# Up projection of a ConvFFN: another order of products, operands, evictions and norm at its border

## The chip, the cores and the metric

The kernel runs on 1 core of one Trainium2 chip. The metric is the device time of one execution in microseconds (us). TensorE (PE, with its weight loads, PEld) multiplies, VectorE (DVE), ScalarE (ACT) and GpSimd (POOL) work elementwise, SyncE (SP) issues most loads. Each engine works through its own queue in order, and semaphores tie the queues together.

## The reference

One layer of a streaming encoder: two kinds of linear attention, an output projection with a residual, a norm, and a gated ConvFFN. The border that this document is on lies between the output projection and the ConvFFN. In 1024 frames of a prompt and 64 of a running stream (T2 = 1088 columns) this is computed there:

```python
x = x + g1 * jnp.einsum('bte,ed->btd', mix, w_out)
h2 = _rmsnorm(x, g_norm_ffn) * (1.0 + sc2) + sh2
a, up = jnp.split(jnp.einsum('btd,df->btf', h2, w_ffn_in), 2, axis=-1)
buf = jnp.concatenate([conv0.astype(a.dtype), a], axis=1)
conv = conv_b + conv_w[0] * buf[:, 0:T]
...
y = jax.nn.silu(conv) * up
x = x + g2 * jnp.einsum('btf,fd->btd', y, w_ffn_out)
```

D_MODEL is 1024, D_FF 2816. All is float32; the kernel gets the precision from matmuls of float32r in three parts (high times high, high times low, low times high), so each operand is cut: ScalarE casts the high half, VectorE subtracts it from the source for the low half (`cut`).

## The kernel before

**Output projection.** The columns are worked off in three chunks (c = 0, 1, 2) of 384, 384 and 320. Chunk by chunk, eight tiles of 128 rows are projected; the result with its residual lies in `hf[0..7]`, eight tiles of 128 x 1088 (in the profile `ab` for 0 to 2, `hf` for 3 to 5, `cv` for 6 and 7). POOL stores each part in DRAM, and the squares are summed in `sqs`.

**Norm.** `norm2` sums the squares over the partitions by a matmul with ones, takes the root on VectorE (`rsqrt`), spreads it over the partitions by three matmuls with the identity, and then scales each tile (VectorE, from PSUM) and adds a bias (ScalarE). It is a generator: for chunks 0 and 1 it runs in steps between the projection's tiles, whenever the program calls `flow.tick()` and a step's delay is over. The chunk that ends last, 2, is normed by explicit calls behind the projection; its columns 256 to 320 have another scale, so each tile takes two instructions on each engine.

**Up projection.** It is a product of blocks with seven products for eight. `hf` is cut in blocks by half of the rows and half of the columns: h11 and h12 are the first and second 544 columns of tiles 0 to 3, h21 and h22 those of 4 to 7. The operands `X[p]` are, in the order of the sums that they need: X1 = h11 and X2 = h21, cut in the norm of chunks 0 and 1; X3 = h22, without a sum; X5 = h12 - h11 (sum 1, in place of h11); X6 = h22 - that (sum 2, in place of h22); X7 = h22 - h12 (sum 3, in place of h12; it must read h22 ahead of sum 2); X4 = (sum 2) - h21 by sum 4, in place of h21. The column at which chunk 1 ends falls into the second half, so sums 1 and 3 have a part of 224 columns that is there after chunk 1 and one of 320 (`edge` to HT) that waits for chunk 2. The 5632 output rows are done in 22 groups q of 2 x 128, the two being of one half each. A product (q, p) is 24 matmuls of 272 columns: four k tiles, three parts, two column halves. Its accumulator is a pair of PSUM banks, `dA` for products 1 and 2, `dX` for the others and for the norm of chunk 2; there are two pairs of each. Products 1 and 2, 6 and 7, 5 and 3 share one accumulator each, and what stands in between is evicted by `evict_in`.

**Weights.** `raw_load` fetches 128 columns of `w_ffn_in` at a time on SP's queue into three buffers; `need_in` forms the weight sums on VectorE and `prep_in` the cut operand of a product, into six slots (`hi` and `lo` by name in turn, whichever half is in them). `prep_to(n)` does that for the first n entries of `steps`.

**Order.** The first entries of `steps` are worked off by a straight list of calls behind the projection, the rest by a loop: prepare weights ahead, `product`, `evict_in`, then parts of the convolution and gate (`run_aux`) within a budget of 2.9 per step. The tiles `ab0` have two buffers; the first one is used for the vectors of the convolution (`ct`, transposed on TensorE in `turn_vectors`), the second and third as the two outputs of q = 0, so that the third takes the first one's place. Each output tile gets two zero columns by POOL when product 1 is evicted.

Of the kernel before, what the change touches and what calls it, by code (L numbers as in the profile page):

```python
# [19 lines left out]
P = 128  # L20
# [173 lines left out]
def stream_step_kernel(  # L194
# [1211 lines left out]
    def sub(out, a, b):  # L1406
        V.tensor_tensor(out=out, in0=a, in1=b, op=ALU.subtract)
# [12 lines left out]
    def parts(c):  # L1420
        return ((0, WID[c], 0),) if c < 2 else ((0, 256, 0), (256, 320, 1))
# [17 lines left out]
    def operand(p, half_k, half_t, pool, a=0, b=HT):  # L1439
        if p not in X:  # L1440
            X[p] = pool.tile([P, 2, 4, HT], F32R, name=f"X{p}", bufs=1)
        t = X[p]
        for i in range(4):
            src = hf[4 * half_k + i][:, half_t * HT + a:half_t * HT + b]
            cut(t[:, 0, i, a:b], t[:, 1, i, a:b], src)
            yield 0.8

    def sums_b(which, a, b, eng=None):

        for i in range(4):  # L1450
            h11, h12 = hf[i][:, a:b], hf[i][:, HT + a:HT + b]
            h21, h22 = hf[4 + i][:, a:b], hf[4 + i][:, HT + a:HT + b]
            if which == 1:
                (eng or V).tensor_tensor(out=h11, in0=h12, in1=h11, op=ALU.subtract)
            elif which == 3:
                sub(h12, h22, h12)
            elif which == 2:
                sub(h22, h22, h11)
            else:
                sub(h21, h22, h21)  # L1460

    def norm2(c, sqs):
# [6 lines left out]
        rstd = rsqrt(vv, 3, "n")  # L1469
        yield 2.5  # L1470
        for j in range(3):
            mm(pn[:, 1, j * P:(j + 1) * P], rstd[:, j:j + 1].broadcast_to([P, P]), ident, True,
               True)
        for k in range(KD):
            for a, b, j in parts(c):
                o = hf[k][:, c * CW + a:c * CW + b]
                V.scalar_tensor_tensor(out=o, in0=o, scalar=A2[:, k, j:j + 1], in1=pn[:, 1, a:b],
                                       op0=ALU.mult, op1=ALU.mult)
                S.activation(out=o, in_=o, func=AF.Identity, bias=B2[:, k, j:j + 1])
            if c < 2:  # L1480
                yield 1.0
            elif k == 3:
                sums_b(1, 2 * CW - HT, HT, G)
        if c < 2:
            yield from operand(1, 0, 0, xap, CW * c, (CW, HT)[c])
            yield from operand(2, 1, 0, xap, CW * c, (CW, HT)[c])
# [84 lines left out]
    for c in range(NC3):  # L1573
# [4 lines left out]
        for n, m in enumerate(M_ORDER[c]):  # L1578
# [112 lines left out]
    def y_sums(q):  # L1691

        i = q // 2
        u0, u1 = abt[q, 0], abt[q, 1]
        b11, b12 = (cvt[i, 0][:, h * 512:h * 512 + 512] for h in range(2))
        b21, b22 = (cvt[i, 1][:, h * 512:h * 512 + 512] for h in range(2))

        def one():
            while small_lo:
# [6 lines left out]
        def two():  # L1706
            sub(u0[:, 512:1024], b22, u0[:, 0:512])
            nc.gpsimd.dma_start(out=d_y[i][:, 4:6], in_=u0[:, 0:1024]
                                .rearrange("p (n t) -> p n t", n=2))
            sub(u1[:, 0:512], u0[:, 512:1024], b21)  # L1710
            nc.gpsimd.dma_start(out=d_y[i][:, 2:4], in_=cvt[i, 1][:, 0:1024]
                                .rearrange("p (n t) -> p n t", n=2))
            nc.gpsimd.dma_start(out=d_y[i][:, 6], in_=u1[:, 0:512])
        aux.extend([("D", one, 1.4), ("D", two, 1.4)])

    def run_aux(budget):
        while aux:
# [22 lines left out]
    def evict_in(q, p):  # L1740
# [103 lines left out]
    prep_to(11)
# [512 lines left out]
```

## Time and profile before

| | us |
|---|---|
| median of 3 runs (1491.54 to 1493.49) | 1491.79 |
| profiled execution, its own time | 1496.77 |
| its span | 1495.0 |
| TensorE busy in the span | 1372.2 (92%) |
| VectorE | 1070.9 (72%) |
| ScalarE | 625.8 (42%) |
| GpSimd | 307.2 (21%) |

All times in the text count from the span's start. The profile tells for each instruction its engine, start and duration, and, where an engine stood idle ahead of it, how long and which engine's work ended that. In names such as `X<-ab,X` the tile written stands ahead of those read. Line 91 is the helper that records every elementwise instruction, line 234 the matmul, line 239 the transpose. PEclk is the share of TensorE's 2.4 GHz that was granted: 1.00 is full clock, 0.50 is 1.2 GHz.

### The profile page before, as it was taken

How to read it: one execution, taken by the hardware profiler on the slowest of the kernel's cores; microseconds unless marked ns; L12 is line 12 of the kernel's file. 1: busy time of each engine (PE TensorE's matmuls, PEld its weight loads, DVE VectorE, ACT ScalarE, POOL GpSimd, SP SyncE). 2: the span in 40 equal slices, each digit the busy share in tenths (PEclk: the TensorE clock that was granted, in tenths of full speed). 3: DMA queues.
4: the chain of work that ended last, by engine and by line, in shares of the span. 5: the costliest groups of instructions: out<-in, count | busy, mean ns of one | idle time of the engine just before them, and what ended most of it. 6: DMA issues, size and time to landing. Idle time of an engine off the chain costs nothing.

```text
span 1495.0 us, 23802 instructions
## 1 busy us (share of the span) xinstructions
PE 1372.2 (92%) x9082; PEld 1277.3 (85%) x9082; DVE 1070.9 (72%) x1992; ACT 625.8 (42%) x1277; POOL 307.2 (21%) x412
## 2 busy tenths in 40 slices
PE   5999888989999998799779999999999999899996
PEld 3788777879988988798769999999999997788875
DVE  6637878967886788646697777777777765568775
ACT  5735434432333223435464444444434444334343
POOL 3335423415242323411110000000000011110010
PEclk9999999999999999899889999999999999999998
DMA  8420102123222222444302422333233338565522
GB/s 255 155 76 4 55 15 75 45 84 100 83 79 86 76 75 62 118 149 139 104 15 72 140 60 76 107 106 98 95 99 106 106 100 289 185 195 184 173 81 113
DMA packets 157977, 158.27 MB, mean 106 GB/s; under 512 B 9738, under 2 KB 128616, under 8 KB 157864
## 3 DMA queue, kind: packets, MB, share of 16 engines
q1 hardware_dynamic: 147303, 120.58, 26.1%
q0 software_dynamic: 10560, 36.18, 7.1%
q8 instruction: 71, 1.16, 0.3%
q14 instruction: 43, 0.34, 0.1%
HBM read 126.80 MB, written 29.93 MB: 105 GB/s over the span
## 4 chain that ended last, share of the span: by engine, by line
PE 56%; DVE 22%; issue 8%; ACT 6%; DMA 2%; POOL 1%; DVEq 0%; ACTq 0%; POOLq 0%
PE dX L234 23%; PE mm L234 10%; PE dA L234 8%; PE mn L234 5%; PE al L234 3%; PE o L234 2%; DVE lo L91 2%; DVE qbd L91 2%; DMA rb<-d_y 2%; DVE acc L91 2%; DVE att L91 1%; ACT hi L91 1%; DVE X L91 1%; PE sc L234 1%; DVE ab L91 1%
## 5 line engine op out<-in xcount | busy, mean ns | idle before, releaser
L234 PE MATMUL dX<-X,lo 128*128 128x272 f32 x1344 | 182.0, 292 | 5.5 <-DVE ab L91 3.4
L234 PEld LDWEIGHTS dX<-X,lo 128*128 128x128 f32 x1344 | 175.6, 191 | 6.6 <-ACT cv L91 3.0
L234 PE MATMUL dX<-X,hi 128*128 128x272 f32 x1296 | 174.8, 291 | 5.0 <-DVE ab L91 2.8
L234 PEld LDWEIGHTS dX<-X,hi 128*128 128x128 f32 x1296 | 168.7, 191 | 5.8 <-issue 2.9
L234 PE MATMUL mm<-act_hi,hi 128*128 128x384 f32 (+1 forms) x480 | 170.8, 356 | 0.3 <-DVE mix L91 0.2
L234 PE MATMUL mm<-act_lo,hi 128*128 128x384 f32 (+1 forms) x480 | 158.9, 331 | 0.1
L234 PE MATMUL mm<-act_hi,lo 128*128 128x384 f32 (+1 forms) x480 | 158.5, 330 | 0.0
L91 ACT CAST hi<-raw 128x512 fp32r<-128x512 f32 (+1 forms) x116 | 91.1, 787 | 78.9 <-DVE raw L91 66.7
L234 PE MATMUL al<-ba,hi 128*128 128x512 f32 x396 | 102.1, 401 | 4.8 <-DVE x L91 4.8
L234 PE MATMUL mn<-lo,hi 128*128 128x512 f32 x396 | 94.6, 395 | 2.7 <-ACT lo L91 2.1
L234 PEld LDWEIGHTS mm<-act_hi,hi 128*128 128x128 f32 x480 | 92.1, 192 | 1.9 <-DVE mix L91 0.5
L234 PEld LDWEIGHTS mm<-act_lo,hi 128*128 128x128 f32 x480 | 91.9, 191 | 0.7 <-POOL act_lo L91 0.3
L234 PEld LDWEIGHTS mm<-act_hi,lo 128*128 128x128 f32 x480 | 91.4, 190 | 0.0
L234 PEld LDWEIGHTS mn<-lo,hi 128*128 128x128 f32 x396 | 74.7, 190 | 19.4 <-ACT lo L91 2.6
L91 DVE SCALAR_TENSOR_TENSOR cv<-ab,cw,cv 128x1088 f32<-128x1088 f32 x44 | 59.3, 1347 | 44.3 <-ACT cv L91 44.3
L234 PEld LDWEIGHTS al<-ba,hi 128*128 128x128 f32 x396 | 72.3, 191 | 20.0 <-DVE x L91 5.9
L234 PE MATMUL mm<-hi,act_hi 128*128 128x256 f32 x288 | 88.3, 307 | 0.3 <-ACT hi L91 0.2
L234 PE MATMUL mm<-lo,act_hi 128*128 128x256 f32 x288 | 82.7, 287 | 3.0 <-DVE lo L91 3.0
L234 PE MATMUL mm<-hi,act_lo 128*128 128x256 f32 x288 | 82.1, 285 | 0.0
L91 POOL TENSOR_TENSOR acc<-acc,prod 128x512 f32<-128x512 f32 x42 | 64.8, 1544 | 81.6 <-ACT prod L91 80.8
L234 PE MATMUL dA<-X,hi 128*128 128x272 f32 x552 | 74.3, 291 | 0.0
L234 PEld LDWEIGHTS dA<-X,hi 128*128 128x128 f32 x552 | 71.8, 191 | 0.0
(352 smaller groups left out, 3091.7 us busy)
## 6 DMA issues: line engine op xcount, KB each, us to landing
raw<-in_w_ffn_in_dram SPq DMA_DIRECT2D x44, 512.0 KB
raw<-in_w_ada_dram SPq DMA_DIRECT2D x32, 512.0 KB
raw<-in_w_in_dram SPq DMA_DIRECT2D x28, 512.0 KB
rw<-in_w_ffn_out_dram SPq DMA_DIRECT2D x51, 256.0 KB
d_y<-cv POOLq DMA_DIRECT2D x22, 512.0 KB, 4.8
rb<-d_y POOLq DMA_DIRECT2D x44, 256.0 KB, 3.8
raw<-in_w_out_dram SPq DMA_DIRECT2D x18, 512.0 KB
wa<-in_w_ada_dram SPq DMA_DIRECT2D x16, 512.0 KB
```

What stands on the lines that cost most here:

```text
L91: return call(*args, **kw)
L234: T.matmul(out, lhsT, rhs, start=start, stop=stop, skip_group_check=more)
```

## The change

The straight list between the projection and the loop is written in another order, and the pieces that it calls are smaller:

- `norm2` falls into `norm_root`, `norm_spread` and `norm_tile`; chunk 2's norm no longer runs as a generator between halves of products.
- `sums_b`, which did four tiles at once, becomes `sum_b` for one tile. `strip(p, i)` makes one tile of an operand: its sum for p = 6 or 4, and its cut.
- The first eight products are (0,1), (1,1), (0,2), (0,3), (0,5), (0,6), (0,7), (0,4) instead of (0,1), (0,2), (1,1), (0,5), (0,3), and the rest. Product (0,3) gets an accumulator of its own, "E", and the eviction of (0,5) adds it.
- The columns `edge` to HT of sum 1 move from POOL to VectorE, those of sum 3 from VectorE to POOL. The parts after chunk 1 are done tile by tile.
- The vectors of the convolution are transposed behind (0,5) instead of in the middle of the first three products.
- Evictions stand ahead of the weights of later products; before the loop weights are made for one product beyond, not three; (0,4) is multiplied in the list, not in the loop; the loop makes two weights at most per step, and in the first sixteen steps one tap of the convolution (cost 1.3 in its budget) is always let through.
- Chunk 0's and 1's norm waits 0.8 instead of 1.0 between tiles, and 0.7 instead of 0.8 between cuts. `y_sums` looks up its tiles when it runs.

```diff
+    def sum_b(which, i, a, b, eng=None):
+        h11, h12 = hf[i][:, a:b], hf[i][:, HT + a:HT + b]
+        h21, h22 = hf[4 + i][:, a:b], hf[4 + i][:, HT + a:HT + b]
+        o, x, y = {1: (h11, h12, h11), 3: (h12, h22, h12), 2: (h22, h22, h11),
+                   4: (h21, h22, h21)}[which]
+        (eng or V).tensor_tensor(out=o, in0=x, in1=y, op=ALU.subtract)
...
+    FIRST = [(0, 1), (1, 1), (0, 2), (0, 3), (0, 5), (0, 6), (0, 7), (0, 4)]
...
+        grp = GROUP[p] if (q, p) != (0, 3) else "E"
+        first = p in (1, 6, 5, 4) or grp == "E"
...
+            if q == 0:
+                V.tensor_tensor(out=view(dst(q, 0, 1)), in0=o, in1=view(dst(q, 0, 1)), op=ALU.add)
...
-    product(0, 1, 0, 2)
-    next(gen)
-    product(0, 1, 2, 4)
-    turn_vectors()
-    evict_in(0, 1)
-    prep_to(6)
-    product(0, 2, 0, 2)
-    all_of(gen)
-    product(0, 2, 2, 4)
-    product(1, 1)
-    all_of(operand(5, 0, 0, xbp))
-    product(0, 5)
-    all_of(operand(3, 1, 1, xbp))
-    evict_in(0, 5)
-    product(0, 3)
-    sums_b(3, edge, HT)
-    sums_b(2, 0, HT)
...
+    def strip(p, i):
+        if p not in X:
+            X[p] = xbp.tile([P, 2, 4, HT], F32R, name=f"X{p}", bufs=1)
+        if p == 6:
+            sum_b(2, i, 0, HT)
+        elif p == 4:
+            sum_b(4, i, 0, HT)
+        half_k, half_t = {5: (0, 0), 3: (1, 1), 6: (1, 1), 7: (0, 1), 4: (1, 0)}[p]
+        cut(X[p][:, 0, i], X[p][:, 1, i], hf[4 * half_k + i][:, half_t * HT:half_t * HT + HT])
...
+    product(0, 1)
+    pn, rstd = norm_root(2, sqs)
+    evict_in(0, 1)
+    need_in(0, 2)
+    product(1, 1)
+    norm_spread(pn, rstd)
+    for i in range(4):
+        norm_tile(2, 4 + i, pn)
+        strip(3, i)
+    product(0, 2)
+    prep_to(4)
+    product(0, 3)
+    for i in range(4):
+        norm_tile(2, i, pn)
+        sum_b(1, i, edge, HT)
+        strip(5, i)
+        sum_b(3, i, edge, HT, G)
+        if i == 0:
+            prep_to(5)
+    evict_in(0, 3)
+    product(0, 5)
     turn_vectors()
...
+    for i in range(4):
+        strip(6, i)
+        if i == 0:
+            prep_to(6)
     evict_in(0, 5)
...
+    product(0, 4)
...
+    prep_to(9)
+    evict_in(0, 4)
...
+    now[0] = len(FIRST) - 1
+    run_aux(1.4)
...
-        cost = prep_to(s + 1 + LA)
+        cost = prep_to(min(n_prep[0] + 2, s + 1 + LA))
...
-        run_aux(2.9 - cost)
+        run_aux(max(2.9 - cost, 1.4 if s < 2 * len(FIRST) else 0.0))
```

In the built order of instructions, TensorE's queue between the projection's last tile and the third product (`ident,ab` is the transpose of the convolution's vectors, `ident,nr` the spread of the norm):

```order
 L239 MATMUL dX<-ident,xr 128x128 x3
-L234 MATMUL dA<-X_7020,hi 128x272 x12
+L234 MATMUL dA<-X_7005,hi 128x272 x24
 L234 MATMUL dX<-ones,sqs 128x1 x3
-L234 MATMUL dA<-X_7020,hi 128x272 x12
-L239 MATMUL dX<-ident,ab_7491 128x88
-L239 MATMUL dX<-ident,ab_7491 128x44
-L234 MATMUL dA<-X_7068,lo 128x272 x12
+L234 MATMUL dA<-X_7005,lo 128x272 x24
 L234 MATMUL dX<-ident,nr 128x128 x3
-L234 MATMUL dA<-X_7068,lo 128x272 x12
```

Whole products stand now on either side of the norm's two matmuls, and the transposes of the vectors are gone from this place.

VectorE's queue where X5 is made, before (the norm of tile 7 of `hf`, the last one, in its two parts, and then X5):

```order
L91 SCALAR_TENSOR_TENSOR cv_6497<-cv_6497,A2_127,dX_7653 128x256 [waits DMASW7_49]
L91 SCALAR_TENSOR_TENSOR cv_6497<-cv_6497,A2_127,dX_7653 128x64
L91 TENSOR_TENSOR X5_7796<-ab_6490,X5_7796 128x544 [waits DMAHW5_49,DMAHW4_49,DMAHW6_49,DMAHW3_49,Activation_49]
L91 TENSOR_TENSOR X5_7796<-ab_6491,X5_7796 128x544 [waits Activation_49]
L91 TENSOR_TENSOR X5_7796<-ab_6492,X5_7796 128x544 [waits Activation_49]
L91 TENSOR_TENSOR X5_7796<-hf_6493,X5_7796 128x544 [waits Activation_49]
```

and after (`hi_7806<-ws` is a low half of the weights):

```order
L91 SCALAR_TENSOR_TENSOR ab_6490<-ab_6490,A2_127,dX_7659 128x256 [waits DMASW2_49]
L91 SCALAR_TENSOR_TENSOR ab_6490<-ab_6490,A2_127,dX_7659 128x64
L91 TENSOR_TENSOR ab_6490<-ab_6490 128x320 [waits Activation_49]
L91 TENSOR_TENSOR X5_7802<-ab_6490,X5_7802 128x544 [waits Activation_49]
L91 TENSOR_TENSOR hi_7806<-ws_7589,hi_7806 128x512 [waits Activation_49]
L91 SCALAR_TENSOR_TENSOR ab_6491<-ab_6491,A2_127,dX_7659 128x256 [waits DMASW1_49]
L91 SCALAR_TENSOR_TENSOR ab_6491<-ab_6491,A2_127,dX_7659 128x64
L91 TENSOR_TENSOR ab_6491<-ab_6491 128x320 [waits Activation_49]
L91 TENSOR_TENSOR X5_7802<-ab_6491,X5_7802 128x544 [waits Activation_49]
```

A tile's scaling, sum and low half follow each other now, and the next tile's scaling stands behind them.

POOL's queue at the same place, after (`ab0_7686` is the second output tile of q = 0; before, the four sums were `ab<-ab` and `hf<-hf`, sum 1):

```order
L91 MEMSET ab0_7684 128x2 [waits Pool_49]
L91 MEMSET ab0_7686 128x2 [waits DMAHW3_49,DMAHW4_49,DMAHW2_49,PE_49]
L91 TENSOR_TENSOR ab_6490<-hf_6494,ab_6490 128x320 [waits DMASW2_49,DVE_49]
L91 TENSOR_TENSOR ab_6491<-hf_6495,ab_6491 128x320 [waits DMASW1_49,DVE_49]
L91 TENSOR_TENSOR ab_6492<-cv_6496,ab_6492 128x320 [waits DMASW0_49,DVE_49]
L91 TENSOR_TENSOR hf_6493<-cv_6497,hf_6493 128x320 [waits DMASW3_49,DVE_49]
```

The sums in this place are now those of sum 3; the fill ahead of them waits for TensorE, that is for the transposes.

## Rows read from the trace of the kernel before

**Rows 1.** Busy us (instructions) of PE, PEld, DVE, ACT, POOL; PEclk, DMA, GB/s

```profile
730.00:745.00 15.00, 9.13 (x42) 8.48 (x41) 9.04 (x28) 4.17 (x10) 1.29 (x4) 0.60 0.09 29
...
760.00:775.00 15.00, 11.80 (x71) 11.40 (x70) 14.93 (x25) 8.54 (x16) 1.22 (x2) 0.77 0.13 36
...
790.00:805.00 15.00, 15.00 (x122) 15.00 (x121) 9.87 (x15) 6.88 (x12) 0.10 (x1) 1.00 0.01 1
```

**Rows 2.** TensorE in order of time: start, us, instruction, count, idle before, releaser

```profile
729.08 1.75 PE L234 MATMUL dA<-X,hi 128*128 128x272 f32 x12
735.77 1.44 PE L234 MATMUL dX<-ones,sqs 128*128 128x1 f32 x6 [4.94 <-DVE sqs L91]
...
739.93 0.61 PE L239 MATMUL dX<-ident,ab 88*128 88x88 f32 x2
...
744.37 0.84 PE L234 MATMUL dX<-ident,nr 128*128 128x128 f32 x3
...
747.61 3.16 PE L234 MATMUL dA<-X,hi 128*128 128x272 f32 x24
...
767.98 5.78 PE L234 MATMUL dX<-X,hi 128*128 128x272 f32 x24 [2.75 <-DVE ab L91]
...
778.43 3.52 PE L234 MATMUL dX<-X,hi 128*128 128x272 f32 x24 [1.50 <-ACT hi L91]
784.74 4.56 PE L234 MATMUL dX<-X,lo 128*128 128x272 f32 x24 [2.79 <-DVE ab L91]
...
798.17 3.17 PE L234 MATMUL dX<-X,lo 128*128 128x272 f32 x24
801.19 3.16 PE L234 MATMUL dA<-X,hi 128*128 128x272 f32 x24
```

**Rows 3.** VectorE in order of time: root of chunk 2 and first scalings

```profile
737.24 0.16 DVE L91 TENSOR_SCALAR vv<-dX 128x3 f32<-128x3 f32 x1 [0.20 <-PE dX L234]
...
739.41 0.16 DVE L91 SCALAR_TENSOR_TENSOR nr<-na,nr 128x3 f32<-128x3 f32 x1
...
745.89 1.84 DVE L91 SCALAR_TENSOR_TENSOR ab<-ab,A,dX 128x256 f32<-128x256 f32 x6 [2.62 <-PE dX L234]
```

**Rows 4.** ScalarE in order of time: the first three tiles' biases

```profile
746.40 2.03 ACT L91 ACTIVATE ab<-ab,B 128x256 f32<-128x256 f32 x6 [3.94 <-DVE ab L91]
```

**Rows 5.** VectorE, 715 to 800, by shape: count, busy us, mean ns, idle before

```profile
L91 DVE TENSOR_TENSOR X<-ab,X 128x544 fp32r<-128x544 f32 x6 | 4.0, 716 | 1.6 <-ACT X L91 1.6
...
L91 DVE TENSOR_TENSOR raw<-raw 128x512 f32<-128x512 f32 x5 | 3.4, 689 | 0.1
...
L91 DVE SCALAR_TENSOR_TENSOR ab<-ab,A,dX 128x256 f32<-128x256 f32 x3 | 1.4, 478 | 2.6 <-PE dX L234 2.6
...
L91 DVE TENSOR_TENSOR ab<-hf,ab 128x320 f32<-128x320 f32 x2 | 0.9, 480 | 0.0
```

**Rows 6.** ScalarE, 715 to 800, by shape, as rows 5

```profile
L91 ACT CAST X<-ab 128x544 fp32r<-128x544 f32 x6 | 3.5, 643 | 0.0
...
L91 ACT ACTIVATE ab<-ab,B 128x256 f32<-128x256 f32 x3 | 1.5, 500 | 3.9 <-DVE ab L91 3.9
...
L91 ACT ACTIVATE ab<-ab,B 128x64 f32<-128x64 f32 x3 | 1.0, 334 | 0.0
```

**Rows 7.** POOL in order of time: second fill and the four sums

```profile
740.61 0.10 POOL L91 MEMSET ab<- 128x2 f32 x1 [4.77 <-PE dX L239]
747.24 2.55 POOL L91 TENSOR_TENSOR ab<-ab 128x320 f32<-128x320 f32 x3 [6.53 <-ACT ab L91]
749.75 0.89 POOL L91 TENSOR_TENSOR hf<-hf 128x320 f32<-128x320 f32 x1
```

**Rows 8.** VectorE in order of time, 601 to 617: alone, then beside POOL's subtractions

```profile
601.48 0.56 DVE L91 TENSOR_TENSOR mix<-mix,gate 128x384 f32<-128x384 f32 x1 [0.96 <-ACT gate L91]
602.30 4.91 DVE L91 TENSOR_TENSOR act_lo<-mix,act_hi 128x384 fp32r<-128x384 f32 x4 [0.26 <-ACT act_hi L91]
```

More of the change, by code (lines that the diff above doesn't have):

```diff
@@ L1445, in operand, with norm_root @@
             cut(t[:, 0, i, a:b], t[:, 1, i, a:b], src)
[L1446 to L1462, printed above, removed]
+            yield 0.7
+    def sum_b(which, i, a, b, eng=None):
[4 more added lines that the diff above has]
+        (eng or V).tensor_tensor(out=o, in0=x, in1=y, op=ALU.subtract)
+    def norm_root(c, sqs):
         pn = pair("dA") if c < 2 else pair("dX")
@@ L1468, in norm2, with norm_spread @@
                         op1=ALU.add)
-        rstd = rsqrt(vv, 3, "n")
-        yield 2.5
+        return pn, rsqrt(vv, 3, "n")
+    def norm_spread(pn, rstd):
         for j in range(3):
@@ L1473, in norm2, with norm_tile @@
                True)
-        for k in range(KD):
[L1475 to L1486, printed above, removed]
+    def norm_tile(c, k, pn):
+        for a, b, j in parts(c):
+            o = hf[k][:, c * CW + a:c * CW + b]
+            V.scalar_tensor_tensor(out=o, in0=o, scalar=A2[:, k, j:j + 1], in1=pn[:, 1, a:b],
+                                   op0=ALU.mult, op1=ALU.mult)
+            S.activation(out=o, in_=o, func=AF.Identity, bias=B2[:, k, j:j + 1])
+    def norm2(c, sqs):
+        pn, rstd = norm_root(c, sqs)
+        yield 2.5
+        norm_spread(pn, rstd)
+        for k in range(KD):
+            norm_tile(c, k, pn)
+            yield 0.8
+        yield from operand(1, 0, 0, xap, CW * c, (CW, HT)[c])
+        yield from operand(2, 1, 0, xap, CW * c, (CW, HT)[c])
         if c == 1:
-            sums_b(1, 0, 2 * CW - HT)
-            yield 1.0
-            sums_b(3, 0, 2 * CW - HT)
+            for i in range(4):
+                sum_b(1, i, 0, 2 * CW - HT)
+                sum_b(3, i, 0, 2 * CW - HT)
+                yield 0.6
     ORD_IN = (1, 6, 5, 2, 7, 3, 4)
-    steps = [(0, 1), (0, 2), (1, 1), (0, 5), (0, 3), (0, 6), (0, 7), (0, 4)]
+    FIRST = [(0, 1), (1, 1), (0, 2), (0, 3), (0, 5), (0, 6), (0, 7), (0, 4)]
+    steps = list(FIRST)
     steps += [(1, p) for p in ORD_IN[1:]]
@@ L1617, in stream_step_kernel @@
                                   .rearrange("j (f p) -> (j f) p", p=P))
-            if c == 2 and n == 5:
+            if c == 2 and n == 6:
                 prep_to(2)
-                need_in(0, 3)
-            if c == 2 and n == 6:
-                prep_to(4)
+                need_in(0, 1)
         if c < 2:
@@ L1694, in y_sums, with blocks @@
         u0, u1 = abt[q, 0], abt[q, 1]
-        b11, b12 = (cvt[i, 0][:, h * 512:h * 512 + 512] for h in range(2))
-        b21, b22 = (cvt[i, 1][:, h * 512:h * 512 + 512] for h in range(2))
+        def blocks():
+            return [cvt[i, n][:, h * 512:h * 512 + 512] for n in range(2) for h in range(2)]
         def one():
+            b11, b12, _, b22 = blocks()
             while small_lo:
@@ L1706, in two @@
         def two():
+            _, _, b21, b22 = blocks()
             sub(u0[:, 512:1024], b22, u0[:, 0:512])
@@ L1725, in run_aux @@
                 last_d[0] = now[0]
+    GROUP = {1: "A", 2: "A", 6: "B", 7: "B", 5: "C", 3: "C", 4: "D"}
     def product(q, p, k0=0, k1=4):
-        grp = {1: "A", 2: "A", 6: "B", 7: "B", 5: "C", 3: "C", 4: "D"}[p]
-        first = p in (1, 6, 5, 4)
+        grp = GROUP[p] if (q, p) != (0, 3) else "E"
+        first = p in (1, 6, 5, 4) or grp == "E"
         if first and k0 == 0:
@@ L1747, in evict_in @@
         have.add(p)
-        o = held[q, {1: "A", 2: "A", 6: "B", 7: "B", 5: "C", 3: "C", 4: "D"}[p]][:, :, 0:HQ]
+        o = held[q, GROUP[p] if (q, p) != (0, 3) else "E"][:, :, 0:HQ]
         cost = 0.75
@@ L1811, in stream_step_kernel @@
     edge = 2 * CW - HT
-    gen = norm2(2, sqs)
-    need_in(0, 2)
-    need_in(0, 4)
-    product(0, 1, 0, 2)
-    next(gen)
-    product(0, 1, 2, 4)
-    turn_vectors()
-    evict_in(0, 1)
-    prep_to(6)
-    product(0, 2, 0, 2)
-    all_of(gen)
-    product(0, 2, 2, 4)
-    product(1, 1)
-    all_of(operand(5, 0, 0, xbp))
-    product(0, 5)
-    all_of(operand(3, 1, 1, xbp))
-    evict_in(0, 5)
-    product(0, 3)
-    sums_b(3, edge, HT)
-    sums_b(2, 0, HT)
-    all_of(operand(6, 1, 1, xbp))
-    evict_in(0, 3)
-    prep_to(7)
+    def strip(p, i):
[7 more added lines that the diff above has]
+        cut(X[p][:, 0, i], X[p][:, 1, i], hf[4 * half_k + i][:, half_t * HT:half_t * HT + HT])
+    prep_to(3)
+    product(0, 1)
+    pn, rstd = norm_root(2, sqs)
+    evict_in(0, 1)
+    need_in(0, 2)
+    product(1, 1)
+    norm_spread(pn, rstd)
+    for i in range(4):
[13 more added lines that the diff above has]
+    product(0, 5)
+    turn_vectors()
+    for i in range(4):
+        strip(6, i)
+        if i == 0:
+            prep_to(6)
+    evict_in(0, 5)
     product(0, 6)
-    all_of(operand(7, 0, 1, xbp))
+    for i in range(4):
+        strip(7, i)
+        if i == 0:
+            prep_to(7)
     evict_in(0, 6)
-    prep_to(8)
     product(0, 7)
-    sums_b(4, 0, HT)
-    all_of(operand(4, 1, 0, xbp))
+    for i in range(4):
+        strip(4, i)
+        if i == 0:
+            prep_to(8)
+    product(0, 4)
     sp = [spp.tile([P, 8, P], F32R, tag="sp", name="sp", bufs=3) for _ in range(3)]
     evict_in(0, 7)
-    prep_to(11)
+    prep_to(9)
+    evict_in(0, 4)
     def spart(f):
```

2 lines of the change are left out of this document (1 added, 1 removed).

## Prediction

> **What bounds the kernel now.** I read the busy shares by stretch first [rows 1]: from 790 us on TensorE is busy all the time at full clock, so whatever the border before it takes is added to the end one for one. In 730 to 745 us TensorE is busy 9.13 of 15 us at a granted 0.60, in 760 to 775 us 11.80 at 0.77, while VectorE is busy 14.93 of 15. The border is therefore VectorE's. Then the matmuls in order of time [rows 2]: product (0,1) begins at 729.08, (1,6), the first of the loop, at 778.43, and (2,1), the first of the third group, at 801.19, behind which products follow each other every 3.02 us. Of these 72.1 us TensorE needs 14 times 3.02, 42.3 us. A wait is dear twice: behind 2.75 us of waiting the 24 matmuls of one product took 5.78 us (the 1.2 GHz level), against 3.16 at 2.4 GHz. The change touches only this stretch; I put it on the same clock, from 729.08 on, and ask when (1,6) and (2,1) begin.
>
> **The start of the norm: earlier by 8.6 us.** Before, the root of chunk 2 begins at 737.24 [rows 3], as its matmul with the ones waited 4.94 us for VectorE, which was making half sums and weights; its spread over the partitions stands behind a half of product (0,2) and comes at 744.37 [rows 2], and the first normed tile at 745.89 [rows 3]. After, the half sums stand some places earlier, in gaps in which VectorE waits for the projection. (0,1) runs 729.08 to 732.4, the ones take 0.7 at full clock (half of their 1.44) to 733.2, and the root takes the 2.35 us of before [rows 3], to 735.6, behind (1,1), which needs no wait and ends at 736.3. With the spread (0.9) the first tile starts at 737.3. TensorE has (0,1), (1,1) and (0,2) done at 740.4, where before it ended the third at 750.8 (747.61 and 3.16).
>
> **The strips: what replaces it.** This is the term that decides. Before, all eight tiles go through VectorE, and ScalarE follows one tile behind: six instructions, three tiles, take 1.84 us [rows 3] and the biases 2.03 [rows 4], so that a tile costs some 0.6 and nobody waits. After, VectorE's queue holds, strip for strip, scaling, (sum,) cut, and each waits for ScalarE's bias or cast of the same strip; both engines work in the order of their queues, so the next strip's scaling can't pass. A strip costs its whole chain, not the larger engine's part. With 0.03 to a hand-over (0.478 [rows 5] from 745.89 ends at 746.37; the bias starts at 746.40 [rows 4]):
> X3: scaling 0.48 (its second part runs beside the first bias), two biases 0.74 (0.50 and 0.33 with the overlap), cast 0.64, low half 0.64 (0.716 less the 0.08 that the next overlaps), hand-overs 0.1 [rows 5, 6]: 2.6, four 10.4, to 747.7.
> Weights of (0,3): difference 0.69, cast 0.62 (by the 0.643 of 544 columns), low half 0.69 [rows 5, 6]: 2.0, to 749.7.
> X5: the same and the sum of 320 columns, 0.48 [rows 5], that now stands on VectorE: 3.1, four 12.4, and the weights' low half 0.6, to 762.7.
> (0,5) does not start with its first strip: its accumulator is the norm's, which the last scaling reads until 760.4. TensorE has stood by then, and I charge it the 5.78 us of the half clock [rows 2]; with the transposes of the vectors (0.6) it ends at 766.8.
> POOL: the fill of the second output tile waits, before as after, for those transposes, since that tile takes their buffer; before, nothing was queued behind it but sums that came 6.53 us later [rows 7]. After, the four sums for X7 stand behind it in POOL's queue, and VectorE's sums for X6 wait for them, as they overwrite what POOL reads. First sum 0.1 and 0.9 later, 767.8: VectorE has idled 5.1 us.
> X6: sum 0.72, cast 0.64, low half 0.64, hand-overs: 2.07, four 8.3, weights 0.6. Beside it run POOL's other three sums. When both engines subtracted at once, four of VectorE's took 4.91 us against 0.56 for one of that width alone [rows 8]; so I add 1.0 (0, if they fit into its waits, to 2.6, three sums of 0.87). To 777.7.
> X7 has no sum, so ScalarE runs ahead: one eviction 0.64, four low halves 2.55, weights 0.6; the eviction of (0,6), two instructions, 1.4. To 782.9.
> X4: like X6, 8.3 and 0.6, to 791.8; eviction of (0,7) 1.4; three sums of weights 2.0; cast and hand-overs 0.65. (1,6) starts at 795.8 against 778.43: **17.4 us later**.
> From below it is 12.3: (0,5) at full clock gives back 2.7, strips without any hand-over 48 times 0.03, POOL's sums the 1.0. From above 22.4: hand-overs of 0.1 add 48 times 0.07, POOL's sums another 1.6.
>
> **The first steps of the loop.** From (1,6) to (2,1) six products took 22.8 us before, 4.6 more than 6 times 3.02: there the weights were late too (2.79 us of waiting ahead of 784.74, then 4.56 us for a product [rows 2]). After, weights are made two to a step, not up to five ahead, and each step must take a tap. From (1,6)'s weights to the eviction that frees the accumulator of (1,4), VectorE has four taps of 1088 columns (1.3 each, twice 0.64), twelve weight instructions (some 0.62), four evictions (0.64) and the seven small ones (1.1): 16.2 us, and waits about 5 for casts and for the convolution's parts on ScalarE: 21.4, against the 19.7 that (1,4) lay behind (1,6). With the half clock for (1,4), 1.4 as at 784.74, that is 3.1 more. Bounds: minus 4.6 (no wait is left) and plus 5.
>
> Moved, and at no cost: the loads of the third and later weights are issued where their buffer comes free and have more time than before, as all is later; chunk 1's shorter pauses fill VectorE's gaps ahead of 729 us, in which TensorE was at the projection's pace (if that cover failed, each 0.1 would be paid once for each tile).
>
> **Sum.** Plus 17.4 plus 3.1: 20.5 us. The profiled execution took 1496.77 (span 1495.0); with it 1517.3. The median of the three is 1491.79, 5.0 below the profiled one; on it the forecast is **1512.3 us**. The parts' own ends are plus 7.7 (12.3 less 4.6) and plus 27.4.
>
> A rule that speaks against my reading: VectorE's four subtractions in 4.91 us [rows 8] beside POOL's. The Trainium skill, "SBUF — State Buffer", section "SBUF: two separate sides", says that a VectorE instruction with two SBUF inputs and a GpSimd one exclude each other for a whole instruction; this trace agrees with it (1.23 us for each instead of 0.56), and by it the term for X6 would be 2.6 rather than 1.0 and the sum 22.1.
>
> **Rivals.** *The strips give work earlier (faster than before).* If the two engines overlapped across strips, a strip would cost VectorE's own part: 1.3 for X3, 1.8 for X5, 1.3 for X6 and X4. X5 would end near 752.8, (0,5) run at full clock, and by the other terms of above (1,6) start at 777.6, 0.8 us sooner; with the loop's 4.6 gone it is 1491.8 less 5.4, **1486**. The place is VectorE's queue between two strips; the sixteen strips of X3, X5, X6 and X4 cost 39.4 us by my count, 2.5 each, and with full clock and no wait in the loop (together 10.4 off 20.5) it turns where their mean falls below 1.8. For it: the norm does come 8.6 us sooner. Against it: the built order, in which each strip's cut is ahead of the next strip's scaling, and VectorE's 14.93 of 15 us [rows 1]. The Trainium skill, "Perfetto Trace Analysis", section "Optimizing Scalar/DVE Operations", says that where these engines are not saturated but cause bubbles elsewhere, breaking up instructions may complete work sooner; that is this rival, and in 760 to 775 us its condition isn't met. 5%.
> *Nothing to be seen (within 0.2%).* X3's and X5's strips overlap (10.4 less), which keeps the full clock for (0,5) (2.7) and leaves no wait in the loop (7.7), and X6's and X4's don't: 20.5 less 20.8, **1491.5**. For and against it stands the same as for the first. 3%.
> *Slower, but half.* Full clock for (0,5) (2.7), and no wait in the loop (3.1 and 4.6), since two weights a step suffice: plus 10.1, **1502**. For it: the wait of 2.79 at 784.74 was of evictions that now come ahead of weights. 12%.
> *Slower by more than 26*, where hand-overs, port and loop all stand at their upper ends: plus 27.4, **1519**. 4%.
>
> **How the numbers follow.** The forecast, slower by 14 to 26, has 76%. A measurement here can tell about 0.2%, 3 us. Faster by more 5%, within it 3%, slower by more 92%. From 1503 to 1518 the range leaves out the faster and the equal case, the lower half of the half case and the last: about 2 in 10.
>
> **What would show it.** In the changed kernel's trace the first normed tile stands near 737 us and the third product's end near 740; then TensorE waits some 9 us for X3. The low halves of X3 follow each other every 2.6 us and those of X5 every 3.1, each behind a wait for ScalarE. POOL's second fill stands behind the transposes, and VectorE waits about 5 us for POOL. (1,6) starts near 796, (2,1) near 822. I am wrong if X3's low halves come every 1.3 us, if (0,5) starts ahead of 757, or if (2,1) starts ahead of 811.

## Result and profile after

| | before | after |
|---|---|---|
| median of 4 runs, us | 1491.66 | 1512.55 (1511.68 to 1513.55) |
| profiled execution, us | 1496.77 | 1511.68 |
| its span, us | 1495.0 | 1509.9 |
| VectorE, ScalarE, GpSimd busy, us | 1070.9, 625.8, 307.2 | 1076.2, 627.1, 307.2 |
| (0,1)'s start to (2,1)'s start, us | 72.1 | 92.8 |

The changed kernel is slower: 1.0136 of the time before, 95% interval 1.0120 to 1.0152, 20.9 us by the medians (of before one more run is in it than ahead of the prediction); in a later group of runs 1.0134 (1.0110 to 1.0158). The spans differ by only 14.9 us. What lies outside of the border explains this: in the profiled execution of before, (0,1) began 2.8 us later (729.08 [rows 2] against 726.29), and the part behind (2,1) took 3.0 us longer (1495.0 less 801.19 against 1509.9 less 819.11). The 2.8 us are not the change's: 2.6 of them are there at the projection's first transposes already, which began at 619.01 and 616.40, and from these to (0,1) the two kernels take 110.1 and 109.9 us. So the border by itself, 20.7 us, is what the medians show, and below every kernel is read by that stretch, from (0,1)'s start to (2,1)'s. To set a time of after beside one of the prediction, add the 2.8.

TensorE in order of time in the changed kernel (start, us, instruction, count, idle before and what ended it), the lines that answer to [rows 2]:

```profile
726.29 3.49 PE L234 MATMUL dA<-X,hi 128*128 128x272 f32 x24
729.99 0.80 PE L234 MATMUL dX<-ones,sqs 128*128 128x1 f32 x6 [0.20 <-DVE sqs L91]
730.65 3.26 PE L234 MATMUL dA<-X,lo 128*128 128x272 f32 x24
733.75 0.83 PE L234 MATMUL dX<-ident,nr 128*128 128x128 f32 x6
734.33 3.25 PE L234 MATMUL dA<-X,hi 128*128 128x272 f32 x24
746.48 5.12 PE L234 MATMUL dX<-X,lo 128*128 128x272 f32 x24 [8.90 <-ACT lo L91]
757.89 4.61 PE L234 MATMUL dX<-X,hi 128*128 128x272 f32 x24 [6.29 <-DVE hf L91]
762.33 0.43 PE L239 MATMUL dX<-ident,ab 88*128 88x88 f32 x2
...
792.33 5.81 PE L234 MATMUL dX<-X,hi 128*128 128x272 f32 x24 [3.33 <-ACT hi L91]
...
814.50 4.77 PE L234 MATMUL dX<-X,lo 128*128 128x272 f32 x24 [4.12 <-DVE ab L91]
819.11 3.17 PE L234 MATMUL dA<-X,hi 128*128 128x272 f32 x24
```

(0,1), the norm's matmul with the ones, (1,1), the spread of the norm and (0,2) now follow each other with hardly a gap, and the third product ends at 737.6. Then TensorE stands for 8.90 us until X3 and the weights of (0,3) are there, for 6.29 us until the norm's accumulator is free for (0,5), for 3.33 us ahead of (1,6) (792.33) and for 4.12 us ahead of (1,4) (814.50). VectorE, in the same kernel, at one strip of X3, one of X5 and the start of X6:

```profile
736.63 0.73 DVE L91 TENSOR_TENSOR X<-hf,X 128x544 fp32r<-128x544 f32 x1 [1.34 <-ACT X L91]
737.28 0.67 DVE L91 SCALAR_TENSOR_TENSOR hf<-hf,A,dX 128x256 f32<-128x256 f32 x2
739.24 0.72 DVE L91 TENSOR_TENSOR X<-hf,X 128x544 fp32r<-128x544 f32 x1 [1.30 <-ACT X L91]
...
757.07 0.67 DVE L91 SCALAR_TENSOR_TENSOR hf<-hf,A,dX 128x256 f32<-128x256 f32 x2
758.36 0.49 DVE L91 TENSOR_TENSOR hf<-hf 128x320 f32<-128x320 f32 x1 [0.62 <-ACT hf L91]
759.57 0.73 DVE L91 TENSOR_TENSOR X<-hf,X 128x544 fp32r<-128x544 f32 x1 [0.72 <-ACT X L91]
763.80 1.36 DVE L91 TENSOR_TENSOR hf<-hf,ab 128x544 f32<-128x544 f32 x1 [3.51 <-POOL ab L91]
765.88 1.41 DVE L91 TENSOR_TENSOR X<-hf,X 128x544 fp32r<-128x544 f32 x1 [0.71 <-ACT X L91]
```

The low halves of X3 stand 2.61 us apart (736.63, 739.24), each behind 1.3 us in which VectorE does nothing. The first matmul of (0,5) comes 0.15 us behind the end of the last scaling (757.07 and 0.67, against 757.89). POOL in the same stretch:

```profile
762.82 0.10 POOL L91 MEMSET ab<- 128x2 f32 x1 [32.86 <-PE dX L239]
762.92 1.67 POOL L91 TENSOR_TENSOR ab<-hf,ab 128x320 f32<-128x320 f32 x2
764.55 1.34 POOL L91 TENSOR_TENSOR ab<-cv,ab 128x320 f32<-128x320 f32 x1
765.86 0.85 POOL L91 TENSOR_TENSOR hf<-cv,hf 128x320 f32<-128x320 f32 x1
```

The fill of the second output tile waited 32.86 us, up to the transposes behind (0,5), and the four sums that stand behind it in POOL's queue waited with it.

### The profile page after: what moved, and what is told of

The parts are those of the page before. It is cut to its first block, busy times and chain, and to the rows that moved or that the text cites. A ratio compares the mean times of both kernels' runs of the same rounds, so it can differ in the third digit from the quotient of the medians.

```text
span 1509.9 us, 23808 instructions
## 1 busy us (share of the span) xinstructions
PE 1370.5 (91%) x9082; PEld 1274.3 (84%) x9082; DVE 1076.2 (71%) x1993; ACT 627.1 (42%) x1277; POOL 307.2 (20%) x412
## 4 chain that ended last, share of the span: by engine, by line
PE 55%; DVE 21%; issue 10%; ACT 5%; DMA 3%; POOL 1%; SPq 0%; DVEq 0%; ACTq 0%; POOLq 0%
PE dX L234 24%; PE mm L234 10%; PE dA L234 8%; PE mn L234 4%; PE al L234 3%; PE o L234 2%; DVE lo L91 2%; DMA rb<-d_y 2%; DVE qbd L91 2%; DVE acc L91 2%; DVE att L91 1%; DVE t L91 1%; PE sc L234 1%; ACT hi L91 1%; DVE X L91 1%
## 5 line engine op out<-in xcount | busy, mean ns | idle before, releaser
L234 PE MATMUL dX<-X,lo 128*128 128x272 f32 x1344 | 187.5, 296 | 18.5 <-ACT lo L91 12.6
L234 PEld LDWEIGHTS dX<-X,lo 128*128 128x128 f32 x1344 | 179.0, 194 | 21.7 <-ACT lo L91 12.9
L234 PE MATMUL dX<-X,hi 128*128 128x272 f32 x1296 | 178.5, 295 | 12.8 <-DVE hf L91 6.3
L234 PEld LDWEIGHTS dX<-X,hi 128*128 128x128 f32 x1296 | 172.4, 195 | 13.5 <-issue 10.0
```

Of the source, the lines that this page charges most:

```text
L234: T.matmul(out, lhsT, rhs, start=start, stop=stop, skip_group_check=more)
```

## Experiments

The stretch from (0,1) to (2,1) is named for each, and the ratio to the kernel before on the same chip. Each edit is made alone and to the changed kernel, unless said otherwise. Two profiles of the changed kernel gave a stretch of 92.8 and 93.6 us, so a difference of less than 1 us in it says little. By the time, of the edits to the changed kernel only numbers 1 and 5 are clear of its own interval (1.0120 to 1.0152); numbers 2, 3, 7 and 9 overlap it and are read by the stretch.

**1. Strips staggered.** The same instructions; the next strip's scaling or sum is ahead of this strip's low half ("h" is the cast, "l" the low half).

```diff
-        norm_tile(2, 4 + i, pn)
-        strip(3, i)
+        if i < 3:
+            norm_tile(2, 5 + i, pn, bias=False)
+        strip(3, i, "h")
+        if i < 3:
+            norm_tile(2, 5 + i, pn, scale=False)
+        strip(3, i, "l")
...
-        strip(6, i)
+    for i in staggered(6):
```

> The changed kernel with the same instructions, but in the strips of X3, X5, X6 and X4 VectorE does the next strip's scaling or sum ahead of the low half of this one, and ScalarE the cast ahead of the next bias. My theory (a strip costs its whole chain through both engines, because their queues are in order): a strip of X3 costs ScalarE's 1.4 instead of 2.6, of X5 VectorE's 1.8 instead of 3.1, of X6 and X4 VectorE's 1.4 instead of 2.07; 4 x 1.2 + 4 x 1.3 + 8 x 0.65 = 15, less about 1.5 for the first and last strips, which still show their chain: 13 to 14 us faster than the changed kernel, about 1499. (0,5) then starts some 9 to 10 us sooner behind (0,1). Rival A (the engines' work itself is too much, VectorE being 14.93 of 15 us busy in the kernel before): the order inside a strip changes nothing, 0 to 2 us, 1511 to 1512.5. Rival B (the loss is TensorE's half clock behind each wait, not the waits): waits get shorter but stay, so the clock does too, 3 us at most, 1509.

Measured: 1498.46 us, 1.0042 (1.0024 to 1.0060); stretch 79.5, 13.3 less. What VectorE waited for up to (1,6), from 726 to 792 in the changed kernel and from 726 to 779 in this one (total us, times, longest; the lines of `X`, `hf` and `ab`):

```profile
DVE X L91 <- ACT X L91: 13.8, 16, 1.3
DVE hf L91 <- POOL ab L91: 3.5, 1, 3.5
DVE ab L91 <- ACT ab L91: 1.9, 3, 0.6
```

```profile
DVE X L91 <- ACT X L91: 2.8, 4, 0.8
DVE hf L91 <- POOL ab L91: 2.1, 1, 2.1
```

Sixteen waits for a cast became four, 13.8 us became 2.8, and the 1.9 for biases went: 12.9 us, about what the stretch lost. Rival A falls, as not one instruction is gone; rival B too, as the time came down although (1,6) met the half clock here as well:

```profile
779.50 5.81 PE L234 MATMUL dX<-X,hi 128*128 128x272 f32 x24 [3.33 <-ACT hi L91]
```

**2. Vectors turned early.**

```diff
     pn, rstd = norm_root(2, sqs)
+    turn_vectors()
     evict_in(0, 1)
...
     product(0, 5)
-    turn_vectors()
```

> The changed kernel with the convolution's vectors transposed right behind the root's matmul with the ones, as early as in the kernel before, so that POOL's fill of the second output tile and the four sums queued behind it don't wait for product (0,5). My theory: VectorE's 3.5 us wait for POOL ahead of X6 goes, and the 1.3 us for which both engines subtracted at once; (0,6) starts 3 to 4.8 us sooner, the time is 1507.5 to 1509.5. Rival (the wait for POOL only covered the wait for the next eviction or for the cast, which are then late themselves): 0 to 1 us, 1511.5 to 1512.5.

Measured: 1508.25 us, 1.0099 (1.0063 to 1.0134); stretch 88.7, 4.2 less. POOL's second fill, and VectorE's first strip of X6:

```profile
726.70 0.10 POOL L91 MEMSET ab<- 128x2 f32 x1 [1.21 <-PE dX L239]
```

```profile
756.51 0.71 DVE L91 TENSOR_TENSOR hf<-hf,ab 128x544 f32<-128x544 f32 x1
757.94 0.73 DVE L91 TENSOR_TENSOR X<-hf,X 128x544 fp32r<-128x544 f32 x1 [0.71 <-ACT X L91]
```

No wait for POOL is left, and sum and low half take 0.71 and 0.73 instead of 1.36 and 1.41.

**3. No forced tap.**

```diff
-        run_aux(max(2.9 - cost, 1.4 if s < 2 * len(FIRST) else 0.0))
+        run_aux(2.9 - cost)
```

> The changed kernel with the loop's old budget (2.9 less the cost of weights and evictions, no tap let through regardless of it). My theory: the forced taps of 1.3 us stand on VectorE ahead of the evictions; without them TensorE's 4.1 us wait and the half clock ahead of the third group (4.77 instead of 3.1 us) are gone: 4 to 5.5 us faster, 1507 to 1508.5. Rival (it is the weights, made two at a time instead of up to five ahead, that are late there): the wait stays, within 1 us, 1512.

Measured: 1509.71 us, 1.0120 (1.0088 to 1.0153); stretch 87.2, 5.6 less, all of it behind (1,6). The changed kernel's VectorE, and this one's TensorE at (1,4):

```profile
802.17 0.69 DVE L91 TENSOR_TENSOR hi<-raw,hi 128x512 fp32r<-128x512 f32 x1 [0.74 <-ACT hi L91]
806.00 1.35 DVE L91 SCALAR_TENSOR_TENSOR cv<-ab,cw,cv 128x1088 f32<-128x1088 f32 x1 [3.13 <-ACT cv L91]
```

```profile
808.84 3.26 PE L234 MATMUL dX<-X,lo 128*128 128x272 f32 x24
811.93 3.16 PE L234 MATMUL dA<-X,hi 128*128 128x272 f32 x24
```

The forced tap stood at the head of VectorE's queue for 3.13 us, for the convolution's part on ScalarE, with the weights and evictions behind it. Without it (1,4) has no wait and full clock. By the medians it is 2.8 us, short of the 4 to 5.5 expected; a wait of 0.99 us came back ahead of a later product, and the rest of the execution differs from run to run (last section).

**4. The early norm alone.** Made to the kernel before: the weights' half sums later, (1,1) between the norm's root and its spread, the norm ahead of (0,2), and everything else operand by operand as before.

```diff
-    need_in(0, 2)
-    need_in(0, 4)
-    product(0, 1, 0, 2)
+    prep_to(3)
+    product(0, 1)
     next(gen)
-    product(0, 1, 2, 4)
     turn_vectors()
     evict_in(0, 1)
-    prep_to(6)
-    product(0, 2, 0, 2)
-    all_of(gen)
-    product(0, 2, 2, 4)
+    need_in(0, 2)
     product(1, 1)
+    all_of(gen)
+    product(0, 2)
+    prep_to(5)
...
     sums_b(3, edge, HT)
+    prep_to(6)
```

> The kernel before with the early half of the change alone: half sums later, root right behind (0,1), (1,1) between root and spread, the norm ahead of (0,2); all eight tiles normed in one go and X5, X3, X6, X4 made operand by operand as before. My theory: the 8.6 us of the earlier norm is mostly lost because TensorE has spent (1,1) and (0,2) by then and stands for X5 while VectorE still has eight tiles, weights and X5 to do (the border is VectorE's); 1 to 4 us faster than the kernel before, 1488 to 1491, and (1,6) about 46 to 48 us behind (0,1). Rival (the norm's start sets the border's end): 8 us faster, 1483 to 1484. Rival (products multiplied early leave nothing to cover the norm): slower, 1493 or more.

Measured: 1489.88 us, 0.9990 (0.9967 to 1.0012), not to be told from the kernel before; stretch 69.2, 2.9 less. TensorE at (1,6) and (1,5):

```profile
773.11 3.51 PE L234 MATMUL dX<-X,hi 128*128 128x272 f32 x24 [2.97 <-ACT hi L91]
779.41 5.78 PE L234 MATMUL dX<-X,lo 128*128 128x272 f32 x24 [2.80 <-DVE ab L91]
```

(1,6) comes 44.9 us behind (0,1) instead of 49.4; the wait for (0,4)'s eviction and the half clock behind it take some of that back. (1,6) is sooner than the 46 to 48 us expected. The norm's 8.6 us are real, but worth no more than the 2.9 in the stretch. Of these 1.1 is given back ahead of it: from the projection's first transposes to (0,1) this kernel takes 111.1 us, where the kernel before took 110.1; 0.84 of it is (0,1)'s wait for its weights.

**5. The three edits together** (1, 2 and 3).

> The changed kernel with all three edits of the runs before it at once: staggered strips, vectors turned early, no forced tap. Alone they took 13.3 (staggered), 4.2 (vectors) and 5.6 us (tap) off the stretch from (0,1)'s start to (2,1)'s, where the change had added 20.7. My theory (these three are the loss, and the early norm is not worth more than a few us): they mostly add up, with some overlap between the first two, since staggering leaves less POOL wait to remove (2.1 instead of 3.5 us): 20 to 22 off, the stretch is 71 to 73 us as in the kernel before (72.1), and the time 1489 to 1493. Rival (a fourth cause of several us is left): 1495 or more. Rival (without the three, the early norm shows its 8.6 us): 1483 to 1485.

Measured: 1491.77 us, 0.9997 (0.9976 to 1.0019); stretch 70.3. The three took 22.5 us off, against 23.1 as the sum of each alone. The stretch is slightly below the 71 to 73 expected. Number 4, which has the early norm and none of the three causes, stands at 69.2; so the three are what the change lost against the kernel before. They are not all that could be lost: number 6, with more of the change's parts, stands at 62.8, and 7.5 us between it and this kernel stay open.

**6. A recombined kernel.** Number 4 (the edit is against it), and three more of the change's parts: the weights of (0,5) ahead of the norm, (0,4) in the list with fewer weights behind it, and its eviction ahead of the other weights.

```diff
-    need_in(0, 2)
+    prep_to(4)
     product(1, 1)
     all_of(gen)
     product(0, 2)
-    prep_to(5)
+    need_in(0, 4)
     all_of(operand(5, 0, 0, xbp))
     product(0, 5)
+    prep_to(5)
...
     all_of(operand(4, 1, 0, xbp))
+    product(0, 4)
...
-    prep_to(11)
+    prep_to(9)
+    evict_in(0, 4)
```

> The kernel before with the early norm in one go, as in the last run of the first group, and three more of the change's parts: the weights of (0,5) ahead of the norm, so that ScalarE can cast X5 right behind the biases; (0,4) in the list, with weights for one product beyond instead of three behind it; (0,4)'s eviction ahead of the other weights. The early norm alone had (1,6) 44.9 us behind (0,1), 4.4 sooner than the kernel before, but then waited 2.80 us for (0,4)'s eviction and paid 5.78 us for a product at half clock. My theory (what pays in the change is the order of evictions and weights, what costs are the strips): that wait goes (2.8 and 2.7), the wait for X5 shrinks by 1 to 2: 3 to 6 us faster than the kernel before, 1485 to 1488. Rival (weights made later are now what is late in the loop): 1490 to 1493.

> The recombined kernel once more, beside the changed one on the same chip. Its stretch from (0,1)'s start to (2,1)'s was 62.8 us against 72.1 in the kernel before, 9.3 less, but its median only 3.9 less, and one execution of code that is the same differs by 4 to 5 us ahead of the border and by 4 behind it. My theory (the 9.3 are real, and the median of ten runs was off by the other parts' scatter): the stretch is 62 to 64 us again, the time 0.994 to 0.998 of the kernel before. Rival (part of the gain is given back behind the border, as the clock in the down projection's entry is lower): 0.998 or more with the same stretch.

> The changed kernel once more on this chip, for the comparison with the recombined one. My theory: the stretch from (0,1) to (2,1) is 92 to 94 us, as in its first profile (92.8), and the time 1.012 to 1.0155 of the kernel before. Rival (the 1.0136 was of that chip and that hour): outside of this.

Measured: 1488.83 us, 0.9976 (0.9958 to 0.9994), stretch 62.8; again, in five rounds, 1489.08 us, 0.9953 (0.9935 to 0.9971), stretch 62.9; the changed kernel beside it 1516.95, 1.0134 (1.0110 to 1.0158), stretch 93.6. This kernel beats both. But of the 9.3 us that its stretch is below the 72.1 of before, the medians show 3.9 and 7.6. Some 1.2 to 1.4 of the rest is lost ahead of (0,1), which waits 0.7 and 0.5 us for its weights and begins 111.2 and 111.5 us behind the projection's first transposes, where it was 110.1 before; what takes the others is open. TensorE at (0,1) and from (0,7) on, in the second of its profiles:

```profile
727.39 3.49 PE L234 MATMUL dA<-X,hi 128*128 128x272 f32 x24 [0.46 <-ACT hi L91]
...
759.85 4.77 PE L234 MATMUL dX<-X,hi 128*128 128x272 f32 x24 [2.74 <-DVE ab L91]
764.46 3.18 PE L234 MATMUL dX<-X,lo 128*128 128x272 f32 x24
770.30 5.04 PE L234 MATMUL dX<-X,hi 128*128 128x272 f32 x24 [2.67 <-ACT hi L91]
775.18 3.18 PE L234 MATMUL dX<-X,lo 128*128 128x272 f32 x24
```

(1,5) at 775.18 follows (1,6) without a wait, as (0,4)'s eviction no longer stands behind weights.

**7 and 8. The price of the half clock.** Matmuls of no use ahead of the waiting products, in the changed kernel (ahead of five products) and in the recombined one (ahead of two).

```diff
+    def fill(q, n):
+        o = held[q, "A"]
+        for _ in range(n):
+            T.matmul(o[:, 0, HQ:512], X[1][:, 0, 0, 0:P], X[1][:, 0, 0, 0:512 - HQ], ...)
...
+        if (q, p) == (1, 6):
+            fill(1, 26)
         product(q, p)
```

> The changed kernel with matmuls of no use put ahead of (0,3), (0,5), (0,6), (0,7) and (1,6) on TensorE's queue (66, 60, 28, 24 and 26 of 240 columns, on X1, into columns that no product reads), so that TensorE works through most of each wait. Everything else is the same. What it tells is the price of the half clock by itself. My theory (the waits are the loss; the half clock is paid only where TensorE is then the late one, in (0,5), 4.61 instead of 3.1, and (1,6), 5.81 instead of 3.1): 3 to 4.5 us faster than the changed kernel, 1508 to 1510. Rival (the half clock is most of the loss): 8 us or more faster, below 1504.5. Rival (the filling lengthens what it stands ahead of): slower than 1513.

> The recombined kernel with 18 matmuls of no use ahead of (0,7) and 20 ahead of (1,6), 240 columns each on X1, into columns that no product reads. In the recombined kernel (0,7) took 4.77 us behind a wait of 2.74 and (1,6) 5.03 behind 2.64, where 3.1 is full clock. My theory (the half clock is paid only where TensorE is late itself, that is in (1,6), behind which products follow without a wait): the stretch is 1 to 2 us shorter than the recombined kernel's, 61 to 62 us; the time is the same within what the runs can tell, 0 to 2 us less. Rival (filling delays the products that it stands ahead of): the stretch is longer, 63.5 or more.

Measured: changed and filled 1510.44 us, 1.0114 (1.0087 to 1.0140), stretch 91.3, 1.6 less; recombined and filled 1489.76 us, 0.9953 (0.9935 to 0.9970), the same as without, stretch 63.9, 1.0 more. By the stretch the first fell short of the 3 to 4.5 us expected, and the second went against my theory. TensorE and VectorE in the second:

```profile
771.92 3.52 PE L234 MATMUL dX<-X,hi 128*128 128x272 f32 x24 [0.74 <-ACT hi L91]
...
789.77 3.29 PE L234 MATMUL dX<-X,lo 128*128 128x272 f32 x24 [2.02 <-DVE ab L91]
```

```profile
783.76 0.69 DVE L91 TENSOR_TENSOR ws<-raw 128x512 f32<-128x512 f32 x1 [2.95 <-DMA raw<-in_w_ffn_in_dram]
```

VectorE without the filling (number 6, second profile), at the same weights and at the eviction ahead of (1,4):

```profile
780.50 0.69 DVE L91 TENSOR_TENSOR ws<-raw 128x512 f32<-128x512 f32 x1 [1.29 <-DMA raw<-in_w_ffn_in_dram]
...
786.49 0.72 DVE L91 TENSOR_TENSOR ab<-ab 128x544 f32<-128x544 f32 x1
```

(1,6) took 3.52 us instead of 5.04, and (1,5) came 1.5 us sooner behind (0,1); but (1,4) then waited 2.02 us for an eviction that stood behind VectorE's wait for the next weights' load. That load was issued 49.1 us behind (0,1) with and without the filling; VectorE could begin on it 5.7 us later with it and 4.0 without, and why, no run shows. So the 1.0 us more came by this load. Nor was there anything to gain: without the filling the eviction ended 59.8 us behind (0,1), just when (1,4) began, and VectorE was at the same place up to the load in both.

In the changed kernel the filling brought (0,3), (0,5), (0,7) and (1,6) to 3.51, 3.26, 3.19 and 3.18 us from 5.12, 4.61, 5.78 and 5.81. VectorE's first sum for X6, which stands behind (0,5), came 1.3 us sooner behind (0,1). (1,6) came only 0.2 sooner, as its weights were cast at 786.83 but the filling held it until 787.92. (1,4) began 2.5 us sooner, behind a wait of 4.62 us instead of 4.12, but took 5.78 instead of 4.77; 1.6 us are left. So a slow product costs time only where VectorE or a later product waits for it, as for (0,5) and (1,6) in the changed kernel; where an eviction or a load is late anyway, a fast one just waits.

**9. Sum 3 on VectorE again.**

```diff
-        sum_b(3, i, edge, HT, G)
+        sum_b(3, i, edge, HT)
```

> The changed kernel with the four parts of sum 3 (columns 224 to 544) on VectorE again, as in the kernel before, and nothing else. POOL's second fill still waits for (0,5) and the transposes, but nothing that VectorE needs stands behind it. My theory: VectorE does 4 x 0.41 us more, but its 3.5 us wait for POOL and the 1.3 us of subtracting at the same time as POOL go; X6 starts 1.5 to 2 us sooner and its first strip is 1.3 shorter, of which part is lost as (0,5) starts 1.2 to 1.6 later: 1 to 3 us faster than the changed kernel, 1509.5 to 1511.5. Rival (moving sum 3 to POOL was a relief for VectorE, the engine that bounds the border): 1 to 2 us slower, 1513.5 to 1514.5.

Measured: 1516.36 us, 1.0153 (1.0123 to 1.0182); stretch 92.1, 0.7 less. The 1 to 3 us of my theory don't show: the time can't be told from the changed kernel's, and the stretch hardly can. VectorE and ScalarE at X6:

```profile
761.93 0.72 DVE L91 TENSOR_TENSOR hf<-hf,ab 128x544 f32<-128x544 f32 x1
766.00 0.73 DVE L91 TENSOR_TENSOR X<-hf,X 128x544 fp32r<-128x544 f32 x1 [3.36 <-ACT X L91]
```

```profile
765.09 0.23 ACT L91 COPY cw<-dX 128x88 f32<-128x88 f32 x1 [3.73 <-PE dX L239]
765.22 0.20 ACT L91 COPY ch<-dX 128x44 f32<-128x44 f32 x1
765.31 0.66 ACT L91 CAST X<-hf 128x544 fp32r<-128x544 f32 x1
```

The sum was done at 762.65, and then its cast waited: on ScalarE's queue the copies of the vectors stand ahead of it, and they need the same transposes that POOL's fill needs. The 3.51 us for POOL became 3.36 us for ScalarE. The place of the transposes is the cause, and it held two queues at once. The Trainium skill, "TensorE: Matmul & The Clock Gate", section "Architectural detail: the array is 16× 32×32, not 1× 128×128", says that ScalarE's and VectorE's queues are strictly first in, first out; these rows agree with it, 3.73 us long.

## Why the prediction was right, point by point

The forecast was 1512.3 us, plus 20.5; measured 1512.55, and plus 20.7 in the stretch. Times below are put on the clock of before (2.8 added).

- **Start of the norm.** Forecast 737.3 for the first scaling, 740.4 for the third product's end; measured 737.4 and 740.4. Right.
- **Strips.** X3 2.6 each, end 747.7: measured 2.61 and 748.0. X5 3.1 each, with the weights to 762.7: measured 3.13 and 763.1. Number 1 shows that the cause is the order in two queues: with the strips staggered the same instructions cost 13.3 us less. The Trainium skill's sentence that breaking up instructions may complete work sooner ("Perfetto Trace Analysis", section "Optimizing Scalar/DVE Operations") is about the size of the pieces; here the same pieces gave 92.8 us in one order and 79.5 in another, so here the order decided.
- **(0,5).** Start 760.4 forecast, 760.7 measured, behind the last scaling, as said. The price of 5.78 us was wrong in this execution, where it took 4.61; in the second profile of the changed kernel it took 5.78. This is a term that one execution doesn't fix.
- **POOL.** Right place, but half of the cause. VectorE waited 3.51 us, not 5.1; of the 1.6 less, 1.2 is (0,5)'s shorter run, and in the second profile, with 5.78 us for (0,5), it waited 4.83. That ScalarE's queue was held by the same transposes is missing in the prediction; number 9 shows it. The sum comes out the same, as the two waits are at the same time.
- **Both engines subtracting.** Forecast plus 1.0 (0 to 2.6); measured 1.36 and 1.41 against 0.72 and 0.73, plus 1.3. VectorE's sum met POOL's second sum, and its low half POOL's fourth; POOL's third stood behind VectorE's sum and took 1.34 instead of 0.85. With the Trainium skill's rule of exclusion ("SBUF — State Buffer", section "SBUF: two separate sides") these rows agree, as each time the instruction that began later took longer by most of what was left of the other. The 2.6 us that the prediction worked out by it did not come, as VectorE met two of POOL's sums and not three.
- **(1,6).** 795.8 forecast, 795.1 measured: plus 16.7 instead of plus 17.4.
- **Loop.** Plus 3.1 forecast, plus 4.0 measured (26.8 against 22.8 us from (1,6) to (2,1)). The forced taps and the waits for ScalarE were named, and number 3 shows them. Not in the sum was (1,6) itself at the half clock, 5.81 us against 3.52 before [rows 2]. It can cover the 0.9: with (1,6) filled to full clock (number 7) the same stretch was 25.4 us, 1.4 less.
- **Sum.** Plus 0.3 at the start of (0,5), minus 1.5 for it and the transposes (4.9 us instead of 6.4), plus 0.5 from X6's first sum to (1,6), plus 0.9 in the loop: the errors are small, but that the total is off by 0.2 only is luck.
- **Rivals.** That the strips overlap and make it faster did not come; with overlap put in by hand (numbers 1 and 5) the stretch is 79.5 and 70.3, and even with all three edits the time is that of before, not 1486.

What stays open: why the recombined kernel's stretch is 7.5 us shorter than that of number 5 (by the medians 2.9 us, on the same chip). Of the 7.5 us 6.1 lie ahead of (0,7), and there VectorE is busy 2.2 us longer in number 5 (31.99 against 29.82) and idle 3.9 us longer. The two kernels differ in sum 1 (POOL or VectorE), in (0,3)'s own accumulator with one more eviction, and in the order of operands; no run parts these.

## What to carry to other kernels

A job cut into strips over two engines with ordered queues costs the whole chain per strip, unless the next strip's first step stands ahead of this strip's last one: count the waits of the one engine for the other (13.8 us here) before and after. When a step is moved, list everything on every queue that waits for it; here one transpose held POOL's sums and ScalarE's casts, and taking away the one alone bought hardly anything (0.7 us). Time that TensorE gains ahead of an eviction or a load that is late anyway is only waited for later.

## What the runs showed of the hardware that was not expected

One execution of the same code differs from the next by more than most of the border's terms. In eight profiles of kernels that are the same up to there, (0,1) began between 721.8 and 726.7 us. Behind the up projection the same wait of 2.1 us was followed by 2.80 us for eleven matmuls in the changed kernel and by 5.06 in number 3:

```profile
1256.37 0.49 PE L234 MATMUL mn<-lo,hi 128*128 128x512 f32 x1 [2.10 <-ACT lo L91]
1257.44 2.80 PE L234 MATMUL mn<-lo,hi 128*128 128x512 f32 x11 [0.58 <-DVE lo L91]
```

```profile
1250.64 0.55 PE L234 MATMUL mn<-lo,hi 128*128 128x512 f32 x1 [2.16 <-ACT lo L91]
1251.71 5.06 PE L234 MATMUL mn<-lo,hi 128*128 128x512 f32 x11 [0.53 <-DVE lo L91]
```

The granted clock was 1.00 behind the first and 0.50 behind the second, after the same matmuls and the same waits. Whether a short wait costs the full clock is not fixed by its length here. A change of a few us is therefore read from its own stretch, and from the median of many runs, not from one time; and as the recombined kernel shows, what a stretch gains need not all be seen in the time.
